# Other banks for single down blocks, activation sums behind weight parts, and keys and values first with keys written twice

## The chip, the cores and the metric

The kernel runs on one core of a Trainium2 chip. The metric is the device time of one execution in microseconds, the median over several runs. Five engines matter here: TensorE (PE in the profile, with its weight loads as PEld), VectorE (DVE), ScalarE (ACT), GpSimd (POOL) and SyncE (SP, which only issues DMAs). Each takes its instructions in order from a queue of its own.

## The reference

One decoder layer in float32 for 256 tokens of width 2048. Cut to its frame:

```python
x = x + 0.5 * swiglu(rms_norm(x, ffn1_norm), w_gate, w_up, w_down)        # width 5632
h = rms_norm(x, mix_norm);  p = h @ w_in
q, k, v, p_rwkv, gates = split(p)       # 1024, 256, 256, 3360, 4096 columns
y_attn = sliding_window_attention(q, k, v, sinks)   # 16 heads of 64, 4 key heads, window 128
y_rwkv = rwkv7_time_mix(p_rwkv, ...)                # a recurrence over the tokens
x = x + (gate_attn * (y_attn @ w_proj_attn) + gate_rwkv * (y_rwkv @ w_proj_rwkv)) @ w_out
x = x + cross_attention(rms_norm(x, cross_norm), mem)
x = x + 0.5 * swiglu(rms_norm(x, ffn2_norm), w_gate, w_up, w_down)
out = rms_norm(x, final_norm)
# swiglu(h) = (silu(h @ w_gate) * (h @ w_up)) @ w_down
```

## The kernel before, in words

**Products.** The weights are read from HBM once and the activations stay on chip. Every float32 factor is held as two rounded parts, high and low, and a product is three matmuls: high by high (L424), high activation by low weight (L425), low activation by high weight (L426). The product is taken in *units* of two chunks of 128 rows of the weight by 512 columns. SyncE loads a unit raw; ScalarE makes its high part by a rounding copy (L341) and VectorE its low part by a subtraction (L342). `next_item` keeps loads up to four units and parts up to two units ahead of TensorE. A unit of a single product (`product`) is 12 matmuls: two chunks, two halves of the tokens (t = 0, 1), three matmuls.

**Pairs.** Where two products share their activation, `product_pair` takes the two weights at once. For some units (q in SEVEN or SEVEN_DOWN) it computes seven block products p1 to p7 in place of eight, after Strassen: this needs sums of weights (`sums`, L348 to L361) and sums of activations. The latter come from `combinations`: VectorE adds and subtracts into u (L453 to L465), ScalarE makes the high part chi or dhi (L468), VectorE the low part clo or dlo (L470). They are made once for each activation, in the background, and used by all pairs that read it.

**Feed-forward.** `feed_forward` cuts the 11 column blocks of 512 into groups of 4, 4 and 3 (GROUPS). In a group come gate and up (block 0 as two single products, the others as pairs), then the group's share of the down product, added to the residual x in place. Down's four column blocks go as two pairs (`down`), except that in the last group only columns 0 and 1 are a pair and columns 2 and 3 are two single blocks (`product`, added at L715). Within `down`, p1 is read by ScalarE (L578), the other results by VectorE in halvings (`half`, L575), and the two combined halves hb and u are added to x as 1024-wide residual sums in the background (L591). In the last group each finished column block n calls `done(n)`: in the first feed-forward that stores it to DRAM by a POOL DMA and starts the next norm's transposes; in the second it sums squares for the final norm.

**PSUM.** Eight banks: three under the tag acc, three under mm, two under tr. Each new tile of a tag takes the next bank in turn and so waits for that bank's last reader. `product` takes two of acc. A pair takes mm for p1, p3 and p5, acc for p2 and p4 (and p8 in `down`), tr for p6 and p7; it asks for each at its first use.

**Mixer.** The columns of w_in come in the order of `weight_plan`: queries 0 to 511, queries 512 to 1023, keys with values, then the recurrence's small columns, its keys, and the rest. Queries are scaled by the norm (`scaled`) and turned to features by `to_features`: transposes on TensorE (`feat`, L606), copies by ScalarE. Attention wants the keys in both halves of the 128 partitions (kd): `keys_values` transposes them, copies them to one half (L810), and has a POOL DMA copy each half to the other (L811). `attend` then runs for each pair of query heads and block of tokens: scores on TensorE (L831, into mm), bias, maximum, exponentials (L856), division (L864), transposes (L870) and their copy (L873), values (L878), parts of the result (L885). It runs in the background, under the product of the small columns and the recurrence's first keys. `decay_and_rate` follows when attention is over: matmuls of the small columns (L950, into mm) and sigmoids (L957).

**Order.** Background work is written as generators in named groups (`Interleave`), and each `bg.tick()` between matmuls advances them by a step; `idle(n)` lets n ticks pass and `wait_for` waits for a name. This gives the program order. A scheduler then sets the order of each engine's queue from it, the dependences, and added edges such as `tc.issue_after(i)`, which puts the instructions under it behind instruction i.

Of the kernel before, what the change touches and what calls it, by code (L numbers as in the profile page):

```python
# [15 lines left out]
P = 128  # L16
# [11 lines left out]
KU = 2  # L28
# [76 lines left out]
def weight_plan(a):  # L105
# [6 lines left out]
    cols = [0, 512, ATTN_W]  # L112
# [27 lines left out]
def decoder_layer(ctx: ExitStack, tc: tile.TileContext, a: dict, out: bass.AP):  # L140
# [161 lines left out]
    raws, parts = {}, {}  # L302
# [32 lines left out]
    def split_raw(raw, pieces):  # L335
        n = raw.shape[2]
        hi = wp.tile([P, KU, n], F32R, tag="hi", name="hi")
        lo = wp.tile([P, KU, n], F32R, tag="lo", name="lo")
        for s, how in pieces:
            with how():  # L340
                act.copy(hi[:, s], raw[:, s])  # L341
            dve.tensor_tensor(lo[:, s], raw[:, s], f32(hi[:, s]), ALU.subtract)  # L342
        return [(hi[:, j, :], lo[:, j, :]) for j in range(KU)]

# [91 lines left out]
    def combinations(sp, x, seven, early, ready, tag, apart):  # L436
# [6 lines left out]
        def work():  # L443
# [4 lines left out]
            for q in sorted(seven + early):  # L448
                while not all(KU * q + i in x.done for i in range(KU)):
# [3 lines left out]
                dve.tensor_tensor(  # L453
                    v[:].rearrange("p k t n -> p k (t n)"), f32(x.at(0, 2 * q, 2)),
                    f32(x.at(1, 2 * q, 2)), ALU.add,
                )
                if q in seven:
                    n = 4
                    dve.tensor_tensor(f[:, 0], v[:, 0, 1], v[:, 1, 1], ALU.add)
                    dve.tensor_tensor(f[:, 1], f[:, 0], v[:, 0, 0], ALU.subtract)  # L460
                    dve.tensor_tensor(f[:, 2], v[:, 0, 0], v[:, 0, 1], ALU.subtract)
                    dve.tensor_tensor(f[:, 3], v[:, 1, 0], f[:, 1], ALU.subtract)
                else:
                    n = 2
                    dve.tensor_tensor(f[:, :2], v[:, :, 0], v[:, :, 1], ALU.subtract)  # L465
                yield from idle(2)
                s = slice(o, o + n)
                act.copy(parts[0][:, s], f[:, :n])  # L468
                yield from idle(2)
                dve.tensor_tensor(parts[1][:, s], f[:, :n], f32(parts[0][:, s]), ALU.subtract)  # L470
# [7 lines left out]
    def product_pair(x: Act, c, w, bank, seven, early, after, end, finish):  # L478
# [8 lines left out]
        b, begun, late = {}, set(), nk // KU - 1  # L487
# [80 lines left out]
    def down(sp, h, c, w, xs):  # L568
# [18 lines left out]
        def residual():  # L587
            for t, v in enumerate((hb, u)):
                yield
                o = xs(t, 0, 2)  # L590
                dve.tensor_tensor(o, v[:].rearrange("p a n -> p (a n)"), o, ALU.add)  # L591
# [5 lines left out]
        product_pair(h, c, w, BANKS | {"p8": acc}, SEVEN_DOWN, (), after, end, finish)  # L597
# [61 lines left out]
    def feed_forward(sp, x, norm: Norm, wg, wu, wd, done, begin_last=lambda: None, last=False):  # L659
# [8 lines left out]
        for gi, (j0, nj) in enumerate(GROUPS):  # L668
# [32 lines left out]
            for n in (0, 2):  # L701
                if n in down_pairs(gi):
                    down(
                        sp, h, d, wd,
                        lambda t, m, w: x[:, t, (n + m) * 512 : (n + m + w) * 512],
                    )
# [61 lines left out]
    with tc.tile_pool(name="mx", bufs=1, reuse_waits="tile") as sp:  # L768
# [32 lines left out]
        kd = t4("kd")  # L801
        vt = t4("vt", (P, 2, KV_W))

        def keys_values():

            b = feat(tok_kv, C4[:2])
            v = kd[:].rearrange("p (c e) t -> p c e t", e=2)
            for e in range(2):
                r, o = slice(64 * e, 64 * e + 64), slice(64 - 64 * e, 128 - 64 * e)
                act.copy(v[r, :, e, :], b[r])  # L810
                pool.dma_start(v[o, :, e, :], v[r, :, e, :])  # L811
            yield
            for t in range(2):
                dve.tensor_copy(vt[:, t, :], tok_kv[:, t, KV_W : 2 * KV_W])
            yield from idle(3)
            bg.seen.add("kv")

        bg.spawn("feat", keys_values())
# [3 lines left out]
        def attend(kv, qb):  # L822
            yield from wait_for("kv")
            w = P * (qb + 1)
# [67 lines left out]
        for kv in range(4):  # L892
            for qb in range(2):
                bg.spawn("attn", attend(kv, qb))


# [619 lines left out]
```

## Time and the profile before

| | us |
|---|---|
| median of 3 runs | 2288.76 |
| lowest and highest run | 2287.34, 2290.76 |
| the profiled execution's own time | 2288.91 |
| its span | 2287.2 |
| TensorE busy | 2258.0 |
| VectorE busy | 1738.3 |
| ScalarE busy | 1216.8 |

Times in a row of the profile are from the start of the span. The span is the time from the first to the last recorded instruction; the execution's own time has 1.7 us around it. The mean granted clock of TensorE over the span is 0.997 of full speed. The two starts of a feed-forward lie near 0 and 1574 us, their last down pairs end near 687 and 2246 us, and attention runs from about 798 to 862 us.

### The profile page before, as it was taken

The numbers are of one execution on the slowest core, as the hardware profiler recorded it, in microseconds if no ns is written. First come the engines' busy times: TensorE is split into PE (matmuls) and PEld (weight loads), VectorE is DVE, ScalarE is ACT, GpSimd is POOL, SyncE is SP. The second block draws the span as 40 slices with busy tenths as digits, with TensorE's granted clock in tenths as the row PEclk, the third lists the DMA queues.
The fourth block names the chain that finished last, engine by engine and source line by source line (L and its number), as shares of the span: only waits on it lengthen the run. The fifth ranks groups of instructions, "written<-read, shape, count | busy, mean of one in ns | idle before, by whom it ended". The sixth has DMA issues, their size and how long they took to land.

```text
span 2287.2 us, 28425 instructions
## 1 busy us (share of the span) xinstructions
PE 2258.0 (99%) x10631; PEld 1847.3 (81%) x10631; DVE 1738.3 (76%) x2116; ACT 1216.8 (53%) x1638; POOL 133.7 (6%) x193
## 2 busy tenths in 40 slices
PE   9999999999999999999999999999999999999998
PEld 7888888888887877778888888887888888888886
DVE  7888988888986477885444466547888888898886
ACT  6555555555555467544444446456555455555554
POOL 2000000000000000200220030001000000000002
PEclk9999999999999999999999999999999999999999
DMA  7665665566665544677533576657665666566664
GB/s 241 199 200 190 198 206 192 186 211 202 197 210 173 165 130 133 197 223 211 148 90 90 159 258 221 202 166 242 195 198 184 205 202 201 191 197 202 202 203 147
DMA packets 223018, 432.79 MB, mean 189 GB/s; under 512 B 17915, under 2 KB 20192, under 8 KB 222880
## 3 DMA queue, kind: packets, MB, share of 16 engines
q1 hardware_dynamic: 214208, 404.80, 55.5%
q0 software_dynamic: 8208, 25.39, 3.5%
q8 instruction: 83, 1.36, 0.3%
q10 hardware_dynamic: 464, 0.79, 0.1%
q14 instruction: 55, 0.45, 0.1%
HBM read 417.56 MB, written 13.11 MB: 188 GB/s over the span
## 4 chain that ended last, share of the span: by engine, by line
PE 86%; DVE 5%; issue 5%; DMA 2%; ACT 2%; SPq 0%; POOL 0%; POOLq 0%; ACTq 0%; DVEq 0%
PE acc L424 18%; PE acc L425 17%; PE acc L426 17%; PE mm L424 7%; PE mm L425 7%; PE mm L426 7%; DVE lo L342 2%; PE tr L606 2%; PE tr L425 2%; PE tr L426 1%; PE tr L424 1%; DMA raw<-in_ffn_w_up_dram 1%; PE mm L1213 1%; ACT hi L341 1%; PE tr L1182 1%
## 5 line engine op out<-in xcount | busy, mean ns | idle before, releaser
L342 DVE TENSOR_TENSOR lo<-raw,hi 128x1024 fp32r<-128x1024 f32 (+1 forms) x770 | 890.2, 1166 | 394.8 <-ACT hi L341 393.7
L341 ACT CAST hi<-raw 128x1024 fp32r<-128x1024 f32 (+1 forms) x770 | 763.6, 1001 | 791.7 <-PE acc L426 389.6
L424 PE MATMUL acc<-hi,xhi 128*128 128x512 f32 (+1 forms) x1196 | 477.7, 400 | 4.2 <-ACT xhi L633 2.2
L425 PE MATMUL acc<-lo,xhi 128*128 128x512 f32 (+1 forms) x1196 | 466.6, 390 | 4.6 <-DVE lo L342 4.6
L426 PE MATMUL acc<-hi,xlo 128*128 128x512 f32 (+1 forms) x1196 | 465.3, 390 | 0.0
L424 PEld LDWEIGHTS acc<-hi,xhi 128*128 128x128 f32 x1196 | 225.4, 189 | 55.0 <-issue 5.7
L425 PEld LDWEIGHTS acc<-lo,xhi 128*128 128x128 f32 x1196 | 225.6, 189 | 52.4 <-DVE lo L342 6.7
L426 PEld LDWEIGHTS acc<-hi,xlo 128*128 128x128 f32 x1196 | 224.9, 188 | 47.7 <-DVE xlo L634 1.1
L360 ACT CAST thi<-raw 128x1024 fp32r<-128x1024 f32 x160 | 165.6, 1051 | 66.9 <-DVE raw L357 33.0
L361 DVE TENSOR_TENSOR tlo<-raw,thi 128x1024 fp32r<-128x1024 f32 x160 | 192.7, 1219 | 1.3 <-ACT thi L360 1.3
L424 PE MATMUL acc<-hi,hhi 128*128 128x512 f32 x452 | 176.9, 394 | 4.3 <-DVE x L575 4.3
L426 PE MATMUL acc<-hi,hlo 128*128 128x512 f32 x452 | 177.3, 392 | 0.0
L425 PE MATMUL acc<-lo,hhi 128*128 128x512 f32 x452 | 177.2, 392 | 0.0
L424 PE MATMUL mm<-hi,xhi 128*128 128x512 f32 x380 | 149.1, 392 | 0.0
L426 PE MATMUL mm<-hi,xlo 128*128 128x512 f32 x380 | 148.1, 390 | 0.0
L425 PE MATMUL mm<-lo,xhi 128*128 128x512 f32 x380 | 148.0, 389 | 0.0
L355 DVE TENSOR_TENSOR raw<-raw 128x1024 f32<-128x1024 f32 x80 | 97.7, 1221 | 24.3 <-DMA raw<-in_ffn_w_up_dram 22.7
L424 PEld LDWEIGHTS acc<-hi,hhi 128*128 128x128 f32 x452 | 85.2, 188 | 23.0 <-issue 2.7
L425 PEld LDWEIGHTS acc<-lo,hhi 128*128 128x128 f32 x452 | 85.2, 188 | 19.3 <-DVE lo L342 2.3
L426 PEld LDWEIGHTS acc<-hi,hlo 128*128 128x128 f32 x452 | 85.2, 188 | 17.3
L425 PEld LDWEIGHTS mm<-lo,xhi 128*128 128x128 f32 x380 | 71.4, 188 | 14.8
L426 PEld LDWEIGHTS mm<-hi,xlo 128*128 128x128 f32 x380 | 71.3, 188 | 14.9
(385 smaller groups left out, 3347.3 us busy)
## 6 DMA issues: line engine op xcount, KB each, us to landing
raw<-in_ffn_w_gate_dram SPq DMA_DIRECT2D x167, 512.0 KB, 3.8
raw<-in_ffn_w_up_dram SPq DMA_DIRECT2D x160, 512.0 KB, 4.7
raw<-in_ffn_w_down_dram SPq DMA_DIRECT2D x152, 512.0 KB, 4.8
raw<-in_w_in_dram SPq DMA_DIRECT2D x136, 512.0 KB, 3.7
raw<-in_w_out_dram SPq DMA_DIRECT2D x32, 512.0 KB, 4.4
raw<-in_ffn_w_down_dram SPq DMA_DIRECT2D x12, 1024.0 KB, 5.1
raw<-in_ffn_w_up_dram SPq DMA_DIRECT2D x8, 1024.0 KB, 5.3
raw<-in_w_proj_attn_dram SPq DMA_DIRECT2D x16, 512.0 KB, 3.7
```

The lines of the kernel that those rows point to most:

```text
L341: act.copy(hi[:, s], raw[:, s])
L342: dve.tensor_tensor(lo[:, s], raw[:, s], f32(hi[:, s]), ALU.subtract)
L355: dve.tensor_tensor(ta[:], raw[:, 1:3], raw[:, 0:2], ALU.subtract)
L360: act.copy(hi[:, s], t[:])
L361: dve.tensor_tensor(lo[:, s], t[:], f32(hi[:, s]), ALU.subtract)
L424: pe.matmul(o, xh, hi, start=first, stop=False, **how)
L425: pe.matmul(o, xh, lo, start=False, stop=False, **how)
L426: pe.matmul(o, xl, hi, start=False, stop=last, **how)
L606: pe.transpose(b[:, o : o + P], tok[:, t, col : col + P], ident[:])
L1182: pe.matmul(b[e][:, m * P : (m + 1) * P], x1[r, j, cs_], x2[r, j, cs_], start=True, stop=True,)
L1213: pe.matmul(vb[:, o : o + P][:, r], lhs(e), rhs[:, r], start=first and e == 0, stop=True, **ek,)
```

## The change

It has three parts.

1. *Banks.* The single down block of column 2 takes its two results from mm instead of acc. `down` asks for its mm banks at its start, in the order p1, p5, p3. Where a single block follows a pair (the last group) the residual sums wait until the pair's last result is read ("halves"), and the calls of `done` for both columns come after them, in the background.
2. *Sums.* `split_raw` remembers the newest high part on ScalarE and the newest low part on VectorE, and every instruction of `combinations` is put behind both.
3. *Keys.* Keys and values are the first product of the mixer. ScalarE writes each key head twice next to each other (kk2) straight from PSUM, and the values too; `to_features` transposes all four column blocks to kd, and the POOL DMAs and VectorE's copies of the values are gone. The attention generators are spawned after the first query product and each waits for keys and for its own queries.

The diff, cut to its core:

```diff
-    cols = [0, 512, ATTN_W]
+    cols = [ATTN_W, 0, 512]
...
             with how():
-                act.copy(hi[:, s], raw[:, s])
-            dve.tensor_tensor(lo[:, s], raw[:, s], f32(hi[:, s]), ALU.subtract)
+                newest["act"] = act.copy(hi[:, s], raw[:, s])
+            newest["dve"] = dve.tensor_tensor(lo[:, s], raw[:, s], f32(hi[:, s]), ALU.subtract)
...
+    @contextmanager
+    def behind_weights():
+        with tc.issue_after(newest["act"].ins), tc.issue_after(newest["dve"].ins):
+            yield
...
-    def product(x: Act, w, skew=False):
+    def product(x: Act, w, skew=False, bank=acc):
...
-        o = [acc() for _ in range(2)]
+        o = [bank() for _ in range(2)]
...
+                with behind_weights():
+                    dve.tensor_tensor(
+                        v[:].rearrange("p k t n -> p k (t n)"), f32(x.at(0, 2 * q, 2)),
+                        f32(x.at(1, 2 * q, 2)), ALU.add,
+                    )
...
-                act.copy(parts[0][:, s], f[:, :n])
+                with behind_weights():
+                    act.copy(parts[0][:, s], f[:, :n])
...
-                dve.tensor_tensor(parts[1][:, s], f[:, :n], f32(parts[0][:, s]), ALU.subtract)
+                with behind_weights():
+                    dve.tensor_tensor(
+                        parts[1][:, s], f[:, :n], f32(parts[0][:, s]), ALU.subtract
+                    )
...
-        b, begun, late = {}, set(), nk // KU - 1
+        b, begun, late = {e: bank[e]() for e in first}, set(), nk // KU - 1
...
         def residual():
+            if then:
+                yield from wait_for("halves")
+                bg.seen.discard("halves")
             for t, v in enumerate((hb, u)):
                 yield
                 o = xs(t, 0, 2)
                 dve.tensor_tensor(o, v[:].rearrange("p a n -> p (a n)"), o, ALU.add)
+            for f in then:
+                yield
+                f()
...
+            if to == "p8" and then:
+                bg.seen.add("halves")
...
+            ("p1", "p5", "p3"),
...
+                        [lambda m=m: done(m) for m in (n, n + 1)] if end else [],
...
-                    if end:
-                        done(n)
-                        done(n + 1)
...
-                    pd = product(h, wd, skew=last and end and m == 3)
+                    pd = product(
+                        h, wd, skew=last and end and m == 3, bank=mm if m == 2 else acc
+                    )
...
-        for h in range(2):
-            tok = scaled(product(n2.x, W["w_in"]), n2.r)
-            qt.append(t4("qt"))
-            bg.spawn("feat", to_features(tok, qt[h], "q"))
-        tok_kv = scaled(product(n2.x, W["w_in"]), n2.r)
...
-                act.copy(v[r, :, e, :], b[r])
-                pool.dma_start(v[o, :, e, :], v[r, :, e, :])
...
         def attend(kv, qb):
             yield from wait_for("kv")
+            yield from wait_for(f"q{kv // 2}")
...
+        pkv = product(n2.x, W["w_in"])
+        kk2 = t4("tok", (P, 2, 512))
+        for t in range(2):
+            act.activation(
+                kk2[:, t, :].rearrange("p (k d f) -> p k d f", k=4, d=2),
+                pkv[t][:, :KV_W].rearrange("p (k f) -> p k f", k=4).unsqueeze(2)
+                .to_broadcast([P, 4, 2, 64]),
+                AF.Copy, scale=n2.r[t],
+            )
+            act.activation(vt[:, t, :], pkv[t][:, KV_W:], AF.Copy, scale=n2.r[t])
+        bg.spawn("feat", to_features(kk2, kd, "kv"))
+        for h in range(2):
+            tok = scaled(product(n2.x, W["w_in"]), n2.r)
+            qt.append(t4("qt"))
+            bg.spawn("feat", to_features(tok, qt[h], f"q{h}"))
+            if h == 0:
+                spawn_attention()
```

More of the change, by code (lines that the diff above doesn't have):

```diff
@@ L1 @@
-from contextlib import ExitStack, nullcontext
+from contextlib import ExitStack, contextmanager, nullcontext
 import concourse.bass as bass
@@ L301, in decoder_layer @@
             items.append((w, k0 + KU * q, c0, n, isinstance(w, tuple) and q in n))
-    raws, parts = {}, {}
+    raws, parts, newest = {}, {}, {}
     at = {"item": 0, "product": 0, "pool": None}
@@ L476, in combinations, with product_pair @@
         return c
-    def product_pair(x: Act, c, w, bank, seven, early, after, end, finish):
+    def product_pair(x: Act, c, w, bank, seven, early, after, end, finish, first=()):
         pw, _, nk, _, n = plan[at["product"]]
@@ L566, in gate_up, with down @@
         return hb
-    def down(sp, h, c, w, xs):
+    def down(sp, h, c, w, xs, then):
         hb = sp.tile([P, 2, 512], F32, tag="hb", name="hb", bufs=2)
@@ L595, in finish @@
             half(xs(t, n, 1), b[to][:], xs(t, n, 1))
-        product_pair(h, c, w, BANKS | {"p8": acc}, SEVEN_DOWN, (), after, end, finish)
+            if to == "p8" and then:
+                bg.seen.add("halves")
+        product_pair(
+            h, c, w, BANKS | {"p8": acc}, SEVEN_DOWN, (), after, end, finish,
+            ("p1", "p5", "p3"),
+        )
     def feat(tok, cols):
@@ L704, in feed_forward @@
                         sp, h, d, wd,
[L705 to L709 removed]
+                        lambda t, m, w, n=n: x[:, t, (n + m) * 512 : (n + m + w) * 512],
+                        [lambda m=m: done(m) for m in (n, n + 1)] if end else [],
+                    )
                     continue
                 for m in (n, n + 1):
[L712 removed]
+                    pd = product(
+                        h, wd, skew=last and end and m == 3, bank=mm if m == 2 else acc
+                    )
                     for t in range(2):
@@ L795, in decoder_layer @@
         qt = []
-        for h in range(2):
-            tok = scaled(product(n2.x, W["w_in"]), n2.r)
-            qt.append(t4("qt"))
-            bg.spawn("feat", to_features(tok, qt[h], "q"))
-        tok_kv = scaled(product(n2.x, W["w_in"]), n2.r)
[L801 to L809, printed above, removed]
-                act.copy(v[r, :, e, :], b[r])
-                pool.dma_start(v[o, :, e, :], v[r, :, e, :])
[L812 to L818, printed above, removed]
         ya = act_tiles("ya", 2)
@@ L890, in attend, with spawn_attention @@
                 bg.seen.add("attn")
-        for kv in range(4):
-            for qb in range(2):
-                bg.spawn("attn", attend(kv, qb))
+        def spawn_attention():
+            for kv in range(4):
+                for qb in range(2):
+                    bg.spawn("attn", attend(kv, qb))
+        kd = t4("kd")
+        vt = t4("vt", (P, 2, KV_W))
+        pkv = product(n2.x, W["w_in"])
[6 more added lines that the diff above has]
+                AF.Copy, scale=n2.r[t],
+            )
+            act.activation(vt[:, t, :], pkv[t][:, KV_W:], AF.Copy, scale=n2.r[t])
[6 more added lines that the diff above has]
+                spawn_attention()
         def shifted(tok, cols, mus, outs, name):
```

23 lines of the change are left out of this document (9 added, 14 removed).

## The prediction

> **What bounds the kernel now.** I read the page first, then TensorE's waits, then a table of windows that shows busy time and granted clock around each wait, and last the timelines of the engines that end those waits. The page:
>
> ```profile
> span 2287.2 us, 28425 instructions
> ...
> PE 2258.0 (99%) x10631; PEld 1847.3 (81%) x10631; DVE 1738.3 (76%) x2116; ACT 1216.8 (53%) x1638; POOL 133.7 (6%) x193
> ...
> PE 86%; DVE 5%; issue 5%; DMA 2%; ACT 2%; SPq 0%; POOL 0%; POOLq 0%; ACTq 0%; DVEq 0%
> ```
>
> TensorE is busy for 99% of the span and carries 86% of the chain that ended last. An edit that takes no matmul away can only win what TensorE loses in waits and in stretches at a lower clock, and can only lose by making new ones. TensorE's waits, each row being what waited, for what, us in total, times, longest:
>
> ```profile
> PE acc L425 <- DVE lo L342: 4.6, 5, 1.9
> PE acc L424 <- DVE x L575: 4.3, 2, 2.2
> ...
> PE mm L831 <- DMA kd<-kd: 1.6, 1, 1.6
> ...
> PE acc L424 <- ACT hi L341: 1.5, 1, 1.5
> ...
> PE mm L950 <- ACT cs L957: 0.9, 1, 0.9
> PE tr L870 <- DVE s L864: 0.7, 2, 0.5
> PE tr L878 <- ACT pt L873: 0.6, 1, 0.6
> ```
>
> Every part of the change has a row here. The windows (length, busy time of PE, PEld, DVE, ACT, POOL, then granted clock, DMA share, GB/s) show what follows a wait:
>
> ```profile
> 685.67:689.08 3.41, 1.29 (x6) 0.95 (x6) 3.41 (x5) 1.04 (x1) 0.00 (x0) 1.00 1.05 393
> 689.08:692.49 3.41, 3.41 (x12) 2.63 (x11) 3.11 (x5) 0.47 (x1) 1.52 (x2) 0.50 1.03 384
> 798.31:801.72 3.41, 1.69 (x14) 1.07 (x14) 1.50 (x4) 0.00 (x0) 0.00 (x0) 1.00 0.94 253
> 801.72:805.13 3.41, 3.41 (x15) 2.68 (x12) 3.28 (x8) 0.47 (x1) 0.00 (x0) 0.50 0.16 59
> 866.57:869.98 3.41, 2.50 (x15) 1.26 (x13) 2.06 (x4) 3.00 (x8) 0.00 (x0) 1.00 0.00 0
> 869.98:873.39 3.41, 3.41 (x11) 2.32 (x12) 2.15 (x4) 2.61 (x7) 0.22 (x1) 0.50 0.00 0
> 1577.40:1581.90 4.50, 1.15 (x4) 0.53 (x4) 4.36 (x10) 3.77 (x5) 0.59 (x1) 1.00 0.86 274
> 2244.00:2247.40 3.40, 1.40 (x6) 1.21 (x7) 3.40 (x5) 1.65 (x3) 0.11 (x1) 1.00 0.58 187
> 2247.40:2250.80 3.40, 3.40 (x16) 2.81 (x16) 3.18 (x5) 3.01 (x7) 3.40 (x2) 1.00 0.33 127
> ```
>
> Three times a stretch of 3.41 us at clock 0.50 follows at once on a stretch of 3.41 us in which TensorE was busy for only 1.29, 1.69 and 2.50 us. TensorE is fully busy in it, so each costs half its length, 1.7 us. Two other waits, near 1580 and 2246, were as long and cost no clock. A short wait can therefore cost nearly twice itself, depending on where it falls.
>
> [...]
>
> **A, other banks for the single block behind a pair.** In the last group the block of column 2 follows a pair at once. It takes its two results from the three acc banks, which the pair's own last results still hold. TensorE:
>
> ```profile
> 687.99 0.47 PE L424 MATMUL acc<-hi,hhi 128*128 128x512 f32 x1 [2.12 <-DVE x L575]
> ...
> 2246.00 0.47 PE L424 MATMUL acc<-hi,hhi 128*128 128x512 f32 x1 [2.15 <-DVE x L575]
> ```
>
> and what ScalarE (first row) and VectorE did at that time in the first feed-forward:
>
> ```profile
> 679.81 0.59 ACT L578 ACTIVATE hb<-mm 128x512 f32<-128x512 f32 x1
> ...
> 683.69 1.29 DVE L575 SCALAR_TENSOR_TENSOR hb<-mm,hb 128x512 f32<-128x512 f32 x2
> 684.89 1.22 DVE L342 TENSOR_TENSOR lo<-raw,hi 128x1024 fp32r<-128x1024 f32 x1
> 686.03 1.22 DVE L591 TENSOR_TENSOR x<-hb,x 128x1024 f32<-128x1024 f32 x1
> 687.16 1.28 DVE L575 SCALAR_TENSOR_TENSOR x<-acc,x 128x512 f32<-128x512 f32 x2
> ```
>
> The reader of acc (687.16) stands behind a residual sum of 1.22 us (L591). After the change the block takes the mm banks of p1 and p5, by the order p1, p5, p3 in which the pair asks for them. Their readers ended at 679.81 + 0.59 = 680.4 and 683.69 + 1.29 = 685.0, before the block's first matmul is due at 685.87 (the wait's end 687.99 less 2.12). Both waits go: 2.12 + 2.15, the waits row's **−4.3**. Next late would be the bank of p3, which the block doesn't take, or the low part of the block's third unit. The residual sums now come behind the pair's last readers, so VectorE's order becomes four halvings, then weight parts, then sums. Laid out by hand with the durations above, the low part ends near 690.2, and is needed two units of 12 matmuls after 685.87: at 0.22 us a matmul (189 in 42.00 us, second row under F) that is 691.2. Covered by 1.0 us. The follow-up work (`done`: a store on POOL's queue, the norm's transposes) moves behind the residual. Nobody reads it until both single blocks are over, 2 × 72 matmuls × 0.22 us = 32 us later, so it costs nothing.
>
> **B, the half-clock stretch at 689.08** follows on that wait. Without the wait its window is full: **−1.7** (0 to −1.7). The second feed-forward had none.
>
> **C, activation sums behind weight parts.** At the start of the second feed-forward:
>
> ```profile
> 1579.07 0.73 PE L424 MATMUL acc<-hi,xhi 128*128 128x512 f32 x2 [1.48 <-ACT hi L341]
> 1581.67 0.50 PE L425 MATMUL acc<-lo,xhi 128*128 128x512 f32 x1 [1.86 <-DVE lo L342]
> ...
> 1575.83 0.62 ACT L468 CAST chi<-u 128x512 fp32r<-128x512 f32 x1 [1.88 <-DVE u L462]
> ...
> 1577.98 1.99 ACT L341 CAST hi<-raw 128x1024 fp32r<-128x1024 f32 x2
> ...
> 1580.39 2.35 DVE L342 TENSOR_TENSOR lo<-raw,hi 128x1024 fp32r<-128x1024 f32 x2
> ```
>
> ScalarE idled 1.88 us for a sum (u), made its high part, and only then the weight's (1577.98). VectorE made sums until 1580.39. With the edges these sums stand behind the newest weight parts, which need no sum: both waits go, 1.48 + 1.86 = **−3.3**. The lower bound on the gain is half, if the sums still come between two units.
>
> **F, what the held sums cost later.** They slide from the first, unpaired products into the first pair, where VectorE has least room:
>
> ```profile
> 59.00:101.50 42.50, 42.19 (x190) 34.61 (x190) 35.89 (x41) 22.81 (x27) 0.00 (x0) 1.00 0.59 193
> 1616.00:1658.00 42.00, 42.00 (x189) 34.51 (x190) 35.51 (x40) 22.57 (x27) 0.00 (x0) 1.00 0.60 192
> ```
>
> VectorE is 85% busy there. The waiting instructions hold what is queued behind them on VectorE and ScalarE, but they wait for weight parts that precede them anyway. The program order after the change shows the sums moved only at the two starts; in the middle groups the order is unchanged, so "behind weights" does nothing there. In the first feed-forward I take **+1.0** (0 to +3: the 6.6 us that VectorE has free in 42.5 hold nearly all of it), in the second 0.
>
> **D, keys and values first, written twice by ScalarE.** Today the keys' other half is copied by a DMA whose landing TensorE awaits:
>
> ```profile
> DMA to landing us min/median/max: 4.0/4.1/4.3
> ...
> 800.23 2.66 PE L831 MATMUL mm<-kd,qt 64*128 64x128 f32 x14 [1.63 <-DMA kd<-kd]
> ...
> 804.66 0.67 ACT L341 CAST hi<-raw 128x576 fp32r<-128x576 f32 x1 [6.57 <-PE acc L426]
> ...
> 808.84 0.88 DVE L864 TENSOR_SCALAR s<-s,den 128x128 f32<-128x128 f32 x4
> ```
>
> No such DMA is left, and the keys lie a whole product (8 units of 12 matmuls, 96 × 0.22 = 21 us) ahead of the first score. The wait goes, **−1.6**, and with it the half-clock stretch at 801.72, **−1.7**. POOL's queue loses two DMAs; SP's only loads these columns in another order; ScalarE's four reads of the result instead of two stand in an engine that is 53% busy.
>
> [...]
>
> **G, transposes.** Keys written twice have four column blocks instead of two: eight transposes instead of four. What four cost:
>
> ```profile
> 1547.74 0.60 PE L606 MATMUL tr<-ident,x 128*128 128x128 f32 x4
> 1548.09 0.48 PE L424 MATMUL acc<-hi,ochi 128*128 128x512 f32 x1
> ```
>
> The next matmul starts 0.35 us after them: **+0.4**.
>
> **H, attention itself** moves: heads 0 to 7 now run under the second query product, the rest under the small columns and the first keys of the recurrence. The first pair's chain from score (800.23) to the end of L864 (809.72) takes 9.5 us. In the new order 28 products stand between scores and transposes: 2.66 + 28 × 0.22 = 8.8 us, so 0.7 us is left bare at worst. For up to two pairs that is what the L870 and L878 rows cost now, 1.3: **0** (±2.5).
>
> **E, decay.** Its matmuls waited 0.9 us for L957 to read a bank (waits row), and the half-clock stretch at 869.98 followed, 1.7: 2.6 in all. In the new order groups of four L950 have 12 products between them and not a second group at once, which covers ScalarE's reads. But the table load ahead of L957 remains. Between 0 and −2.6 I take the middle, **−1.3**.
>
> **Sum:** −4.3 − 1.7 − 3.3 + 1.0 − 1.6 − 1.7 + 0.4 + 0 − 1.3 = −12.5 us. The profiled execution took 2288.91 us, 0.15 above the median of the runs shown, so no correction: **2276.4 us**.
>
> **Rivals.**
> *The half-clock stretches stay.* [...] Other small waits, moved by some us, can fall badly instead. Then B, D's stretch and E give nothing (−4.7 becomes 0): 2281.1 us. [...] Against: the new order leaves no wait of 2 us that I can see. Chance 0.18.
> *VectorE is late anyway.* It was 3.41 of 3.41 us busy beside both waits of A. If the weight's low part is next late, A and B give nothing, and C gives half: 2276.4 + 6.0 + 1.7 = 2284.1 us. Against: the 1.0 us of slack worked out in A. For: it is thin. Chance 0.15.
> *Attention under a full product, slower.* Under the second query product VectorE and ScalarE also make weight parts of 1.2 and 1.0 us each, where now they make those of 288 columns. If one such part gets ahead of each of the chain's three hops (VectorE, ScalarE, VectorE), the chain is 9.5 + 1.2 + 1.0 + 1.2 = 12.9 us against 8.8 covered: 4.1 us for each of four pairs, and after each a half-clock stretch of 1.7: 23.2 more, 2299.6 us. It decides the sign from (12.5 + 4.6) / 4 = 4.3 us a pair, stretch included. For: VectorE's load there. Against: a part of 0.67 us (804.66) stood in the chain before, and it cost 1.3 us in all. Chance 0.09.
> That the edges in part C do nothing where the order is unchanged is in the sum already.
>
> **How the numbers follow.** Forecast 0.58, and the rivals 0.18, 0.15 and 0.09. A measurement of this kernel tells about 0.2%, 4.6 us, from no change: faster is below 2284.2, slower above 2293.3. The forecast and the first rival are faster, apart from 0.04 in their tails. The second rival sits on the bound, half on each side. The third is slower in two of three cases. Faster 0.79, same 0.14, slower 0.07. The range: down to 2271.5, where E gives all (−1.3), H 2.5 and F nothing (−1.0); up to 2285.0, which takes in the first two rivals and leaves the third out.
>
> **What would show it.** In the profile after: the rows L575 and kd<-kd gone from TensorE's waits (A, D); hi L341 gone, and lo L342 3 us at most (C); no clock of 0.50 near 687, 800 and 870 (B, D, E); L870 and L878 together under 4 us (H); no wait over 1 us between 45 and 100 us (F). The forecast is wrong if lo L342 grows, if stretches at 0.50 sit behind L870, or if a wait near 688 remains under another name.

## The result and the profile after

The changed kernel takes 2272.34 us (median of 4 runs, 2270.65 to 2273.84) against 2289.76 us for the kernel before (4 runs, 2287.34 to 2293.14): a ratio of 0.9923, 95% interval 0.9905 to 0.994. That is 17.4 us less; 2276.4 us was forecast. The profiled execution took 2270.65 us. Its page:

```profile
span 2268.9 us, 28433 instructions
...
PE 2252.7 (99%) x10635; PEld 1847.8 (81%) x10635; DVE 1735.9 (77%) x2114; ACT 1214.1 (54%) x1638; POOL 131.4 (6%) x191
...
PE 96%; DVE 2%; issue 1%; ACT 1%; DMA 0%; POOLq 0%; POOL 0%; ACTq 0%; SPq 0%; DVEq 0%
```

TensorE's share of the chain that ended last rose from 86 to 96%, and the DMA's fell from 2 to 0. TensorE's waits (what waited, for what, us in total, times, longest); of the changed kernel L429 to L431 are the three matmuls of a product, L584 is the pair's halving, L603 the residual sum, L461 to L477 are the activation sums:

```profile
PE acc L430 <- DVE lo L342: 1.9, 1, 1.9
PE acc L429 <- ACT xhi L653: 1.4, 1, 1.4
PE tr L430 <- DVE tlo L366: 1.1, 1, 1.1
PE mm L185 <- POOL ones L181: 1.1, 1, 1.1
PE tr L868 <- DVE s L862: 0.8, 1, 0.8
PE mm L1060 <- DVE lt L1066: 0.6, 2, 0.4
PE tr L876 <- ACT pt L871: 0.6, 1, 0.6
PE tr L1213 <- DVE mk L1204: 0.2, 1, 0.2
```

The rows that the change aimed at are gone: the pair's reader (4.3), the keys' DMA (1.6), hi L341 (1.5), cs (0.9). lo L342 fell from 4.6 in five waits to one of 1.9. The windows show full clock where TensorE stood at half before, near 687. Near 800 and 870 the clock is full too; the trace has one new stretch at half clock near the start, after the wait on xhi (L653), and no other while TensorE has work:

```profile
8.44:11.86 3.42, 3.42 (x9) 2.67 (x9) 2.31 (x5) 1.85 (x4) 1.72 (x4) 0.52 1.03 361
683.50:687.00 3.50, 3.50 (x17) 2.92 (x16) 3.50 (x6) 1.06 (x1) 0.00 (x0) 1.00 1.04 398
687.00:690.40 3.40, 3.40 (x17) 2.77 (x17) 3.40 (x4) 1.25 (x2) 0.00 (x0) 1.00 0.95 348
```

To see where the time went, I number the 512-wide matmuls in TensorE's queue (8904 in each trace) and compare the start of the same number in two traces, at boundaries of whole products. The times in the heads are those of the kernel before; each cell is what a kernel's profiled execution gains on the profiled execution before within that region, in us (negative: it loses). The first region begins with the first of these matmuls.

| kernel | to 673: first feed-forward | 673–750: its last down blocks | 750–1334: mixer | 1334–1564 | 1564–1650: start of the second | 1650–2230 | 2230 to end: last down blocks |
|---|---|---|---|---|---|---|---|
| changed kernel | 1.0 | 4.1 | 6.2 | 0.0 | 4.1 | 0.4 | 2.4 |
| changed kernel again (e4) | -0.1 | 4.1 | 6.3 | 0.0 | 4.1 | -0.4 | 2.4 |
| e1 banks part alone | -0.9 | 4.1 | 3.2 | -0.1 | -1.4 | 0.4 | 2.4 |
| e2 sums part alone | 0.2 | 1.6 | -0.3 | 0.0 | 4.1 | -1.0 | 0.0 |
| e3 keys part alone | -1.1 | 0.0 | 6.2 | 0.0 | -1.8 | 0.5 | -1.6 |
| e5 residual behind, acc | -0.4 | 4.1 | 4.6 | -0.3 | 4.1 | -0.1 | 2.4 |
| e6 banks, residual ahead | 0.4 | 4.2 | 6.4 | -0.1 | 4.1 | -0.1 | 1.1 |
| e7 only ScalarE's sums behind | 0.5 | 4.1 | 4.7 | 0.0 | 3.6 | -0.2 | 2.4 |
| e8 only VectorE's sums behind | 0.3 | 4.1 | 4.8 | 0.0 | 4.1 | 0.4 | 2.4 |
| e9 keys first, by DMA | 1.1 | 4.1 | 6.7 | -0.1 | 4.1 | -0.8 | 2.4 |
| e10 keys last, written twice | 0.3 | 4.1 | 3.1 | -0.1 | 4.1 | 0.6 | 2.4 |
| e11 attention later | 0.1 | 4.1 | 5.5 | 0.0 | 4.1 | 0.7 | 2.4 |
| e12 inversion's steps behind weights | 0.0 | 4.1 | 8.5 | -0.2 | 4.1 | 0.0 | 2.4 |

### The profile page after: what moved, and what is told of

It is laid out like the page before. It is cut to its first block, busy times and chain, and to the rows that moved or that the text cites. A ratio compares the mean times of both kernels' runs of the same rounds, so it can differ in the third digit from the quotient of the medians.

```text
span 2268.9 us, 28433 instructions
## 1 busy us (share of the span) xinstructions
PE 2252.7 (99%) x10635; PEld 1847.8 (81%) x10635; DVE 1735.9 (77%) x2114; ACT 1214.1 (54%) x1638; POOL 131.4 (6%) x191
## 4 chain that ended last, share of the span: by engine, by line
PE 96%; DVE 2%; issue 1%; ACT 1%; DMA 0%; POOLq 0%; POOL 0%; ACTq 0%; SPq 0%; DVEq 0%
PE acc L429 20%; PE acc L430 20%; PE acc L431 20%; PE mm L431 8%; PE mm L429 8%; PE mm L430 8%; PE tr L626 2%; PE tr L430 2%; PE tr L431 2%; PE tr L429 2%; PE mm L1230 1%; PE tr L1199 1%; DVE lo L342 0%; PE mm L829 0%; ACT hi L341 0%
## 5 line engine op out<-in xcount | busy, mean ns | idle before, releaser
L341 ACT CAST hi<-raw 128x1024 fp32r<-128x1024 f32 (+1 forms) x770 | 763.6, 1000 | 781.6 <-PE acc L431 389.4
L342 DVE TENSOR_TENSOR lo<-raw,hi 128x1024 fp32r<-128x1024 f32 (+1 forms) x770 | 892.4, 1169 | 375.3 <-ACT hi L341 374.2
L429 PE MATMUL acc<-hi,xhi 128*128 128x512 f32 (+1 forms) x1196 | 478.0, 400 | 1.4 <-ACT xhi L653 1.4
L431 PE MATMUL acc<-hi,xlo 128*128 128x512 f32 (+1 forms) x1196 | 465.1, 389 | 0.0
L429 PEld LDWEIGHTS acc<-hi,xhi 128*128 128x128 f32 x1196 | 225.2, 188 | 50.7 <-issue 5.4
L431 PEld LDWEIGHTS acc<-hi,xlo 128*128 128x128 f32 x1196 | 224.9, 188 | 47.8 <-DVE xlo L654 0.9
L430 PE MATMUL acc<-lo,hhi 128*128 128x512 f32 x404 | 158.1, 391 | 0.0
L431 PE MATMUL acc<-hi,hlo 128*128 128x512 f32 x404 | 158.0, 391 | 0.0
L429 PE MATMUL acc<-hi,hhi 128*128 128x512 f32 x404 | 157.4, 392 | 0.0
L429 PE MATMUL mm<-hi,xhi 128*128 128x512 f32 x380 | 149.3, 393 | 0.0
L431 PE MATMUL mm<-hi,xlo 128*128 128x512 f32 x380 | 148.3, 390 | 0.0
L430 PEld LDWEIGHTS acc<-lo,hhi 128*128 128x128 f32 x404 | 75.9, 188 | 17.4 <-DVE lo L342 2.3
L429 PEld LDWEIGHTS acc<-hi,hhi 128*128 128x128 f32 x404 | 75.9, 188 | 15.9 <-DVE x L584 0.9
L431 PEld LDWEIGHTS acc<-hi,hlo 128*128 128x128 f32 x404 | 75.9, 188 | 15.4
L431 PEld LDWEIGHTS mm<-hi,xlo 128*128 128x128 f32 x380 | 71.3, 188 | 14.7
```

The costliest lines, as they stand in the source:

```text
L341: newest["act"] = act.copy(hi[:, s], raw[:, s])
L342: newest["dve"] = dve.tensor_tensor(lo[:, s], raw[:, s], f32(hi[:, s]), ALU.subtract)
L429: pe.matmul(o, xh, hi, start=first, stop=False, **how)
L430: pe.matmul(o, xh, lo, start=False, stop=False, **how)
L431: pe.matmul(o, xl, hi, start=False, stop=last, **how)
```

## The experiments

Every edit of e1 to e3 is a part of the change put into the kernel before; e5 to e12 edit the changed kernel. Medians are of 4 to 11 runs.

### The three parts alone, and the whole again (e1 to e4)

```diff
# e1_banks: of the change's diff only the lines of product, product_pair, down and its calls
+        b, begun, late = {e: bank[e]() for e in first}, set(), nk // KU - 1
+                yield from wait_for("halves")
+                        h, wd, skew=last and end and m == 3, bank=mm if m == 2 else acc
# e2_sums: only newest, behind_weights and its uses
+                with behind_weights():
# e3_keys: only the column order, kk2, and the place of attention
+    cols = [ATTN_W, 0, 512]
+        bg.spawn("feat", to_features(kk2, kd, "kv"))
+                spawn_attention()
# e4_after_again: no edit
```

> The kernel before with the banks part alone (mm banks for the single block of column 2, p1, p5, p3 asked for at the start, residual sums and the follow-up work behind the pair's last results). Theory (three separate costs): both waits on L575 at the last down pair go, 2.1 us each, and the half-clock stretch behind the first: about 6.0 us less than before, 4.06 in the first feed-forward and 2.4 in the second as the trace of the whole change has them. Rival (clock by alignment): only the waits go, 4.3 us, and a stretch at 0.50 turns up behind another wait. Nothing else in the trace moves.

> The kernel before with the activation sums put behind the weight parts alone. Theory: the start of the second feed-forward gives about 4.0 us (waits on hi L341 and lo L342, 1.48 + 1.86, and the wait on L606 after them), and the start of the first gives about 1 us, as in the trace of the whole change (waits at 59 and 113 us gone): about 5 us less. Rival (the prediction's step F): the sums held back cost 1.0 us in the first pair of the first feed-forward: about 2.3 us less.

> The kernel before with the keys part alone (keys and values first, keys written twice by ScalarE, attention from the first query product on). Theory: the wait on the keys' DMA (1.6) and the half-clock stretches at 802 and 870 (1.7 each) and the wait on L957 (0.9) go, less some transposes: about 6 us less, all of it between 750 and 1320 us. Rival (clock by alignment): the stretches reappear behind other waits of the mixer, and only 2 to 3 us are gained.

> The changed kernel once more, unaltered, for a second profile. [...]

Measured, each against the kernel before (21 runs, 2290.69 us): banks 2281.19 us, ratio 0.9966 (0.9953 to 0.9978); sums 2284.97, 0.9974 (0.9965 to 0.9983); keys 2286.68, 0.9984 (0.9975 to 0.9993); the whole 2272.58, 0.9923 (0.9909 to 0.9936). The three gains in medians, 9.5, 5.7 and 4.0, add up to 19.2, and the whole gains 18.1: within what these runs can tell, the parts are separate costs.

The table has more. Each part gives its gain in its own region to 0.1 us: the banks 4.1 and 2.4, the sums 4.1, the keys 6.2, the same as in the whole. But regions that a part doesn't touch move too, by steps near 1.7: e1 gains 3.2 in the mixer, and loses 1.4 at 1564. Those are half-clock stretches that come and go. TensorE waits just as long in e1 as before: 1.56 us for the keys' DMA and 0.92 us for cs, yet no window there is below 1.00, while a stretch now stands at 1575, a wait that cost no clock before; e3 has three, all behind waits that it shares with the kernel before. The windows of e1 (first row) and e3:

```profile
1575.05:1578.46 3.41, 3.13 (x8) 2.52 (x9) 3.38 (x5) 0.45 (x2) 0.00 (x0) 0.52 0.62 201
```

```profile
690.43:693.84 3.41, 3.41 (x12) 2.67 (x11) 3.03 (x5) 0.47 (x1) 1.52 (x2) 0.54 0.98 362
1577.59:1581.00 3.41, 3.41 (x10) 2.63 (x9) 3.09 (x5) 1.08 (x2) 0.00 (x0) 0.50 0.64 189
2243.40:2246.80 3.40, 3.40 (x10) 2.60 (x10) 2.67 (x4) 1.50 (x5) 3.35 (x2) 0.53 0.40 154
```

So a wait of 0.9 to 2.2 us costs half of 3.41 us more in some executions, in others not. The mean granted clock of each run shows it too: of the 21 runs of the kernel before, the 11 at clock 0.995 took 2290.2 to 2293.8 us, and the 5 at 0.997 took 2287.2 to 2289.0.

The starts of the stretches in one trace lie whole multiples of 3.413 us apart: 33.0 and 20.0 of them between 689.08, 801.72 and 869.98 in the kernel before, 260.0 and 195.0 between 690.14, 1577.61 and 2243.21 in e3. The half-clock stretch after the last matmul starts 467.0 of them behind 689.08 in the kernel before. One wait shows both outcomes, that of 1.85 us on lo L342 near 961 us, which the changed kernel still has. Its rows in e5, the second being the stretch, then in e9, the second starting 382.0 of them ahead of the half-clock stretch after the last matmul there (2264.86):

```profile
960.86:964.27 3.41, 1.56 (x7) 1.00 (x6) 3.20 (x10) 1.05 (x1) 0.00 (x0) 1.00 0.34 120
964.27:967.69 3.42, 3.42 (x9) 2.65 (x8) 2.49 (x6) 0.56 (x1) 0.00 (x0) 0.50 0.80 214
```

```profile
957.55:960.97 3.42, 1.85 (x9) 1.19 (x7) 3.04 (x13) 1.05 (x1) 0.42 (x1) 1.00 0.41 156
960.97:964.38 3.41, 3.14 (x14) 2.61 (x15) 3.34 (x8) 0.54 (x1) 0.00 (x0) 1.00 0.59 154
```

In e5, e7 and e8 the wait lies whole in one such row, TensorE is busy for 1.56 to 1.58 us of its 3.41, and the next row is at half clock. In e3, e4, e6, e9 and the changed kernel the wait is split between two rows, none is busy for less than 1.85 us, and the clock stays full. What decides whether a stretch follows is not shown: 1.69 us of busy time in 3.41 were followed by one (798.31, before), 1.49 us in e2 (684.21) were not.

In e4 the stretch near 8 us of the changed kernel is missing, but the kernel isn't shorter by it at the next boundary. Without the stretch, TensorE waits a second time for xhi (two waits, 1.8 us); with it, once (1.4 us). At the start a half-clock stretch shows no cost: of the profiles with the sums part, the three that have it (changed kernel, e2, e5) gain 1.0, 0.2 and -0.4 us in the first region, the eight without it -0.1 to 1.1. That the input is late anyway is the likely reason; no run separates it.

### What takes the wait at the last down pair away: the bank or the residual's place (e5, e6)

```diff
# e5_defer_only
-                        h, wd, skew=last and end and m == 3, bank=mm if m == 2 else acc
+                        h, wd, skew=last and end and m == 3, bank=acc
# e6_banks_only
         def residual():
-            if then:
-                yield from wait_for("halves")
-                bg.seen.discard("halves")
             for t, v in enumerate((hb, u)):
```

> The changed kernel, but the single block of column 2 takes acc again, as before; residual sums and follow-up work stay behind the pair's last results. The prediction's theory (part A: the bank decides): the block waits again for a reader of acc, about 0.9 us less than before because one residual sum of 1.22 us no longer stands ahead, so two waits of about 0.9 us, 2 us slower than the changed kernel. Rival (the residual's place decides): with the residual sums gone from in front, the reader of p2 in acc ends at 683.4 as in the trace after, 2 us before the block is due, and no wait over 0.3 us remains: the time of the changed kernel within 0.5 us.

> The changed kernel, but the residual sums are made at once again, ahead of the pair's last readers; the single block keeps the mm banks of p1 and p5. The prediction's theory (the bank decides): no wait at the block's start, the time of the changed kernel within 0.5 us. Rival (the residual's place decides): a low part of the weight or the next column's acc is late behind the sums, and a wait of 1 us or more returns near 687 and 2230 under another name: 2 us or more slower.

Measured: e5 2273.97 us (2272.92 to 2274.29), e6 2273.6 (2272.53 to 2275.7); the kernel before, beside them, 2290.78. In the table e5 has both gains in full, 4.1 and 2.4, with acc for the single block as before. So the residual's place takes both waits away without the other bank; the order p1, p5, p3 and the place of `done` stayed in e5 and were not tried apart. VectorE in the changed kernel shows why, beside its rows before the change (686.03, 687.16):

```profile
682.73 0.69 DVE L584 SCALAR_TENSOR_TENSOR x<-acc,x 128x512 f32<-128x512 f32 x1 [0.19 <-PE acc L431]
683.34 1.28 DVE L584 SCALAR_TENSOR_TENSOR hb<-mm,hb 128x512 f32<-128x512 f32 x2
684.53 1.21 DVE L342 TENSOR_TENSOR lo<-raw,hi 128x1024 fp32r<-128x1024 f32 x1
685.66 0.69 DVE L584 SCALAR_TENSOR_TENSOR x<-acc,x 128x512 f32<-128x512 f32 x1
...
687.46 1.22 DVE L342 TENSOR_TENSOR lo<-raw,hi 128x1024 fp32r<-128x1024 f32 x1
688.59 2.36 DVE L603 TENSOR_TENSOR x<-hb,x 128x1024 f32<-128x1024 f32 x2
```

The reader of the first acc bank now runs at 682.73, ahead even of p5's two halvings. Before, it ran at 687.16, behind a weight part and a residual sum. With it early, acc is free before the block's start near 686. In e5, where the block does take acc, the same reader stands at the same place, and the block starts without a wait at 687.30:

```profile
684.10 0.69 DVE L584 SCALAR_TENSOR_TENSOR x<-acc,x 128x512 f32<-128x512 f32 x1 [0.20 <-PE acc L431]
```

The medians of e5 and e6 lie 1.0 to 1.6 us above those of the changed kernel (2272.34, 2272.58), more than the 0.5 us of the expectations. In e5's profile the loss is elsewhere: 1.6 us in the mixer, where the stretch behind the wait near 961 stands, and the scatter of the first region. In e6's it is a wait in the second feed-forward, told next.

The banks without the residual's move (e6) take the first wait away too (4.2), but in the second feed-forward only 1.1 of 2.4 remain: the wait there turns into one of another name, on the low part that now stands behind the residual sums. That wait among e6's:

```profile
PE mm L430 <- DVE lo L342: 1.1, 1, 1.1
```

and VectorE in the first feed-forward of e6, where the same order just fits:

```profile
685.63 1.22 DVE L600 TENSOR_TENSOR x<-hb,x 128x1024 f32<-128x1024 f32 x1
686.76 1.28 DVE L584 SCALAR_TENSOR_TENSOR x<-acc,x 128x512 f32<-128x512 f32 x2
687.96 1.21 DVE L600 TENSOR_TENSOR x<-hb,x 128x1024 f32<-128x1024 f32 x1
...
690.29 1.22 DVE L342 TENSOR_TENSOR lo<-raw,hi 128x1024 fp32r<-128x1024 f32 x1
```

That low part ends at 691.5, against 688.7 in the changed kernel.

### Which engine's sums made the start of the second feed-forward late (e7, e8)

```diff
# e7_sums_act: VectorE's instructions of combinations (twice)
-                with behind_weights():
+                with nullcontext():
# e8_sums_dve: ScalarE's copy alone
-                with behind_weights():
+                with nullcontext():
                     act.copy(parts[0][:, s], f[:, :n])
```

> The changed kernel with only ScalarE's part of the sums (L475 of the changed kernel) behind the weight parts; VectorE's sums are free again. If ScalarE's place decides at the start of the second feed-forward (it waited 1.88 us for a sum ahead of the weight's high part): the wait on hi L341 stays away, and of the 3.3 us there about half comes back through lo L342. If VectorE's place decides: both waits come back, 3.3 us slower. If ScalarE's decides alone: nothing comes back.

> The changed kernel with only VectorE's sums behind the weight parts; ScalarE's rounding of the sums is free again. If VectorE's place decides: neither wait comes back, since a sum that is made late can't hold ScalarE early. If ScalarE's place decides: the wait on hi L341 (1.5 us) comes back near 1565.

Measured: e7 2273.76 us (2273.64 to 2274.43), e8 2272.92 (2271.59 to 2274.06). In the region from 1564 on e8 gains all of 4.1 and e7 3.6. Neither hi L341 nor lo L342 makes TensorE wait there. Either edge is enough. That fits the sums being a chain between the two engines, where one held link holds the rest. ScalarE in the changed kernel, then in e7:

```profile
1562.51 2.10 ACT L341 CAST hi<-raw 128x1024 fp32r<-128x1024 f32 x2
...
1569.96 0.62 ACT L474 CAST chi<-u 128x512 fp32r<-128x512 f32 x1
```

```profile
1564.43 2.11 ACT L341 CAST hi<-raw 128x1024 fp32r<-128x1024 f32 x2
1566.44 0.62 ACT L474 CAST chi<-u 128x512 fp32r<-128x512 f32 x1
```

In both, the weight's two high parts come straight after the norm, ahead of the sum's. Before, ScalarE idled 1.88 us for u and made chi first. With only ScalarE held, VectorE still makes u first (from 1564.63), but the weight's high parts are there by 1566.5, and their low parts (1567.02) run ahead of the sum's (clo, 1569.29). The 4.7 and 4.8 of e7 and e8 in the mixer hold the stretch behind the wait near 961. The half microsecond that e7 lacks is a wait on hb at 1602.9, 0.4 us idle and 0.66 between starts.

### What the keys part consists of (e9 to e11)

```diff
# e9_keys_dma: keys and values first, then as before
+        tok_kv = scaled(pkv, n2.r)
...
+                act.copy(v[r, :, e, :], b[r])
+                pool.dma_start(v[o, :, e, :], v[r, :, e, :])
# e10_keys_last: queries, queries, then keys written twice
-    cols = [ATTN_W, 0, 512]
+    cols = [0, 512, ATTN_W]
# e11_attend_later
-            if h == 0:
+            if h == 1:
                 spawn_attention()
```

> The changed kernel with keys and values first, but the keys' other half written by the POOL DMA as before (four transposes less). If the order alone takes the wait away (the landing of 4.1 us lies under a product of 21 us): no wait on the keys' DMA, the time of the changed kernel within 0.5 us, up to 0.4 us faster by the four transposes. Rival: the doubled writing is needed, and a wait on the DMA comes back.

> The changed kernel with the products in the old order (queries, queries, keys and values), the keys written twice by ScalarE without a DMA, attention from the end of the third product on, as before. If the DMA's landing was the whole cost: the wait at the first score falls from 1.6 us to under 0.5 us and the mixer is as long as in the changed kernel, but for L957's wait of 0.9 us near 865. If the order matters too: the chain of copy, eight transposes and copy is bare at the first score for 1 us or more.

> The changed kernel with attention spawned after the second query product instead of the first, so that it runs under the small columns and the first keys again. Separates attention's new place from the keys' order. Part E of the prediction (decay's matmuls no longer back to back because attention is over earlier): the wait of 0.9 us on L957 comes back, 1 to 2.6 us slower with its clock. If it does not come back, something else of the change took it away. Attention's own waits (L868, L876: 1.4 us in the changed kernel) fall to the 1.3 us of before or lower.

Measured: e9 2271.06 us (2270.39 to 2273.11), e10 2273.25 (2271.48 to 2274.76), e11 2273.05 (2272.15 to 2273.2). No wait on the keys is left in any of them. The order alone hides the DMA (e9), and e9 gains 0.5 us more in the mixer than the changed kernel. Its edit leaves out four transposes, forecast at 0.4; its other copies are not separated from them. The doubled writing alone (e10) needs no order. What comes back in e10 and e11, with attention at its old place, is decay's wait; the waits of e10, then of e11:

```profile
PE mm L966 <- ACT cs L973: 1.4, 2, 1.1
```

```profile
PE mm L1060 <- DVE kk L1041: 0.9, 1, 0.9
...
PE mm L967 <- ACT aa L974: 0.5, 1, 0.5
...
PE mm L967 <- ACT cs L974: 0.3, 1, 0.3
```

So decay's wait hangs on where attention ends, as part E has it, and the keys' wait on either of the two other edits. e10's loss in the table, 3.1 us, holds one half-clock stretch, at 915.0, behind two of the recurrence's waits of 0.5 and 0.4 us (L1059); e11's is 0.7 and has none.

### A wait that stayed: the triangular inversion ahead of a weight part (e12)

The largest wait left, 1.86 us, lies in the mixer. VectorE in the changed kernel, with TensorE's row last:

```profile
957.56 0.15 DVE L1088 TENSOR_TENSOR tmp<-xt,dl 128x1 f32<-128x1 f32 x1
...
960.53 0.22 DVE L1088 TENSOR_TENSOR tmp<-xt,dl 128x64 f32<-128x64 f32 x1
960.67 1.22 DVE L342 TENSOR_TENSOR lo<-raw,hi 128x1024 fp32r<-128x1024 f32 x1
```

```profile
961.94 0.50 PE L430 MATMUL acc<-lo,xhi 128*128 128x512 f32 x1 [1.86 <-DVE lo L342]
```

From 957.56 to 960.67 VectorE makes small steps of the inversion, one behind the other, while the low part that TensorE wants next stands in the queue behind them. That is the pattern of the activation sums, so the same edge was put there:

```diff
             for t in range(1, 32):
-                dve.tensor_tensor(
+                with behind_weights():
+                    dve.tensor_tensor(
...
-                dve.tensor_reduce(xt[:, :t, t], tmp[:, :t, :t], AX.X, ALU.add)
+                with behind_weights():
+                    dve.tensor_reduce(xt[:, :t, t], tmp[:, :t, :t], AX.X, ALU.add)
```

> The changed kernel with the same edges (behind the newest weight parts) on the small VectorE steps of the triangular inversion in the recurrence (a multiplication and a sum of 128 lanes by up to 32 x 32 for each of 31 rows). In the trace after, a low part of the weight stands behind 3 us of these steps near 960 us, and TensorE waits 1.86 us. If the edges act there as at the feed-forward's start: that wait goes, 1.9 us faster, 3.5 us at most with a half-clock stretch. Rival: the steps are then late for the work that waits for the inverse, and as much comes back there.

Measured: 2269.31 us (2268.37 to 2270.01), ratio to the kernel before 0.9907 (0.9894 to 0.9921). All its runs lie below all 9 runs of the changed kernel (2270.65 to 2273.84, median 2272.58): 3.3 us less, with the kernel before at 2290.39 beside it and at 2290.69 beside e4. The wait on lo L342 is gone, and the mixer gains 8.5 where the changed kernel gains 6.2. The medians gain more than the 2.3 us between these two profiles; a stretch follows this wait in three of the eight profiles that have it at 1.8 to 1.9 us (changed kernel, e3 to e9), but not in the profile of the changed kernel. What remains of TensorE's waits in the mixer of e12:

```profile
PE tr L868 <- DVE s L862: 0.8, 1, 0.8
PE mm L1060 <- DVE lt L1066: 0.6, 2, 0.4
PE tr L876 <- ACT pt L871: 0.6, 1, 0.6
PE tr L1215 <- DVE mk L1206: 0.2, 1, 0.2
```

Of the kernels run this is the shortest. Together with e9's DMA it might give 0.5 us more; that was not tried.

## Why the prediction was right, and where its steps were off

The direction, the engine and the places were right: each region in which it forecast a gain gave time, and the others moved within their scatter. By its steps, in one profiled execution each:

| step | forecast | measured | from |
|---|---|---|---|
| A + B, last down blocks | -6.0 | -6.5 | 4.1 + 2.4 |
| C, start of the second feed-forward | -3.3 | -4.1 | table |
| F, sums held back in the first pair | +1.0 | -0.5 | below |
| D + G + H + E, mixer | -4.2 | -6.2 | table |

**A was right in its size, and half wrong in its reason.** The prediction let the bank decide, and put the residual's move down as a change in VectorE's order that had to be covered. e5 shows that the move does it without the bank, and e6 that the bank without the move falls 1.3 us short in one of two places. VectorE's order as laid out by hand was wrong in one point: the reader of the first acc bank went ahead of p5's halvings instead of behind them, and the low part ended at 688.7, not 690.2.

**B took one draw for a property.** The stretch at 689 went with its wait. But e2 has the same wait of 2.1 us without the stretch, e3 has it again, and has one at 2243 where the kernel before had none. The term for a wait's clock is a chance: of the five places (689, 802, 870, 1577, 2244), each in the three profiles of the kernel before and e1 to e3 that have its wait, 9 of 15 have the stretch. And the kernel before had more than its profiled execution showed: its median over 21 runs is 2290.69, 1.8 us above that execution. The first rival (stretches that stay and only move) was right in part. At the three places that the change cleared, no stretch is left, since there is no wait to follow; behind the wait near 961, which stayed, one does come in e5, e7 and e8.

**C was 0.8 us short, because idle time is not the whole of a wait.** The prediction summed idle times of 1.48 and 1.86 us. TensorE in the kernel before:

```profile
1577.20 0.39 PE L426 MATMUL acc<-hi,xlo 128*128 128x512 f32 x1
1579.07 0.73 PE L424 MATMUL acc<-hi,xhi 128*128 128x512 f32 x2 [1.48 <-ACT hi L341]
```

The starts are 1.87 us apart, and 0.23 without a wait: 1.64 us are lost for 1.48 of idle time. The second wait cost 2.03 for 1.86. The four transposes near 1615.5 cost another 0.2, 1.11 us between the products around them against 0.90 in the changed kernel: 3.9 of the 4.1. The same holds for A, where the two waits cost 2.28 and 2.31 between starts; with the stretch of 1.7 that is 6.3 of the 6.5. In the window from 1540 to 1660 us the changed kernel has no wait at all.

**F had the wrong sign.** It priced the held sums by VectorE's busy share of 85%, without asking what filled the rest. In the first pair VectorE itself was waiting for weights; the rows before, and after:

```profile
57.45 1.22 DVE L355 TENSOR_TENSOR raw<-raw 128x1024 f32<-128x1024 f32 x1 [0.58 <-DMA raw<-in_ffn_w_up_dram]
```

```profile
57.20 0.69 DVE L461 TENSOR_TENSOR u<-xhi,xlo 128x512 f32<-128x512 f32 x1
57.80 0.75 DVE L713 SCALAR_TENSOR_TENSOR hb<-acc,rs,hb 128x512 f32<-128x512 f32 x1
```

The sums went into that gap, and the wait on hb at 59.39 us (0.3 of idle time) is gone in every profile with the sums part. From the matmul that is due at 45 us to the one at 105 us, which takes in the first pair, all 11 profiles with the sums part gain 0.47 to 0.56 us; e1 and e3, without it, -0.07 and 0.00. The whole region to 673 us scatters more: over the 11 profiles it gains 0.3 us on average (-0.4 to 1.1); the three without it lie at 0.0, -0.9 and -1.1. That the arrival of weights sets the rest of this scatter, through the wait on tlo near 113 us, is argued from its rows and was not tested.

**Mixer: E was halved, and a row was left unread.** D's wait and stretch (3.3) are gone, and G's 0.4 fits the 0.5 that e9 gains. E took half of 2.6; all of it went, and e11 brings 0.8 us of it back by attention's place alone. H held: L868 and L876 together wait 1.4 us after, 1.3 before. The rest is the row lo L342. The prediction used 1.86 us of its 4.6, and the other 2.7 lie in the mixer:

```profile
PE acc L425 <- DVE lo L342: 2.7, 4, 1.3
```

These four waits became one of 1.9. The wait on ga (0.5) went too. The slower rival, attention under a full product, didn't come about: parts of up to 1.2 us did get into the chain (three L342 between 821.5 and 824.9 us in the changed kernel), but TensorE waits once for a softmax there, 0.8 us at 827.84 (twice before, 0.7 in all), and no stretch follows.

**The range held with 0.8 us to spare, in part by luck.** Its lower end, 2271.5, was reached with E whole, F at nothing and 2.5 us from H. E came whole, but H gave nothing. In its place stood terms that the range did not contain: F's 0.5 of gain, 0.8 more from C, 0.5 more from A and B, and in the mixer the rest of lo L342 (0.8) and ga (0.5).

## What to carry to other kernels

When a busy engine waits for a buffer's reader, look first at what stands ahead of that reader in its engine's queue: moving work that nobody waits for behind it took both waits away without another bank. An edge that puts optional work behind the newest part that the bottleneck engine needs paid at both starts of a feed-forward (0.5 and 4.1 us), and again where the change hadn't put it (e12). A wait of one or two us on TensorE should be priced between starts, plus a chance of 1.7 us (9 of 15 of the waits above had it), and a single profile shows only one draw of that chance.

## What the runs showed of the hardware

While TensorE has work, the half-clock stretches in these traces last 3.41 us at 0.50. Where a trace has several, they start whole multiples of 3.413 us apart (33.0 and 20.0 in the kernel before, 260.0 and 195.0 in e3). The same wait has a stretch behind it in one execution and not in another: near 961, TensorE was busy for 1.56 of the 3.41 us before the stretch in e5, and for 1.85 and 3.14 in the two rows over the wait in e9, which has none. Stretches came after waits as short as 0.9 us (869.98 in the profile before), and in e10 after two of 0.4 and 0.5 us (915.0). Single executions of one kernel spread by 6.6 us (2287.15 to 2293.77 over 21 runs) where this kernel had the five waits of 689, 802, 870, 1577 and 2244, and by 3.2 us (2270.65 to 2273.84 over 9 runs) after the change took them away. At the start a stretch showed no cost (1.0, 0.2 and -0.4 us gained with it, -0.1 to 1.1 without).
